# Softmax rows copied by DMA and transposed as fp32r in a hybrid SSD and chunk-band attention step

## The chip, the cores and the metric

The kernel runs on one core of one Trainium2 chip, as a single launch. The metric is the device time of that launch in microseconds (us). The figure before the change is the median of three runs.

## What is computed

One inference step of a two-layer encoder, for 1024 prompt frames and 64 sample frames with a model width of 1024. Layer 0 is a Mamba-2 SSD mixer and a SwiGLU feed-forward part; layer 1 is chunk-band attention and a second SwiGLU part. All arrays are float32. The part that the change touches is the attention of layer 1 (16 heads of 64; chunks of 64 frames; a frame sees its own chunk and the 8 before it):

```python
def band_attend(q, k, v, qpos, kpos, rel_bias):
    dist = jnp.clip(qpos[:, None] - kpos[None, :], -REL_CLIP, REL_CLIP) + REL_CLIP
    bias = rel_bias[:, dist].astype(jnp.float32)
    ...
    s = jnp.einsum('bqhd,bkhd->bhqk', q, k).astype(jnp.float32) * (ATT_HEAD_DIM ** -0.5) + bias
    s = jnp.where(valid, s, -jnp.inf)
    p = jax.nn.softmax(s, axis=-1).astype(v.dtype)
    return jnp.einsum('bhqk,bkhd->bqhd', p, v)
```

## The kernel before

Activations lie with the features on the 128 partitions and the 1088 frames (1024 + 64) along the row. Weights and activations of the large matmuls are split into a rounded fp32r part and its remainder, and each product is made of three fp32r matmuls (L533 to L535 in `passes`).

**The attention stage.** Heads go in pairs, j = 0 to 7, and the frames of a pair in nine blocks of 128 queries, b = 0 to 8 (`att_task(j, b)`, L1975; block 8 is the 64 sample frames, whose keys are mostly the cached ones). A block's keys are 128, 256, 384 and 512 wide for b = 0 to 3 and 640 wide for b = 4 to 8; `w_` is that width and `nkt = w_ / 128`. A block runs in three parts:

- *scores* (L1995 to L2019), for the two heads e = 0 and 1: TensorE writes the scores into a PSUM tile `S` (L2001, L2002, fp32r), VectorE adds the bias and keeps the minimum of the negated scores (L2011), ScalarE takes the exponential and its sum (L2016), VectorE multiplies by the reciprocal (L2017, L2018). The result is the tile `sc` in SBUF, 128 queries by `w_` keys, of which there are four;
- *transposes* (L2028 to L2037): for each head `nkt` transposes of 128 x 128 into a PSUM tile `ptp` (L2032, fp32, with the identity `ident`), which shares its two buffers with `S`; then VectorE (e = 0) or ScalarE (e = 1) copies it to `pT` (L2036);
- *values* (`values`, L2050): the product with V (L2067), made for three blocks at a time, just before the transposes of every third block; the result goes to a DRAM scratch through the tile `ot`.

The keys, values and queries of the next pairs are projected in between (`units`, with `passes`; `evk`, `evq` and `evv` split the results; the lower half of a query remainder is brought to the other partitions by a small DMA, L1942).

**The order of the work.** TensorE's instructions stand in the order in which the program makes them. That order is laid by the class `Stream`: a clock `st.t` advances by the estimated cost of what is issued, and side tasks such as `att_task` are generators that give back a cost, a delay and a condition. `st.pump()`, called between parts of the projection matmuls, lets a side task go on once its delay is over and its condition holds. If the main loop has to wait (`wait_for`), the clock advances by 0.25 at a time without any matmul. After the scores a block's task yields with

```python
yield 1.1 * w_ / 640, AT_W1, lambda: (
    cur["B"] == seqn and st.t >= cur["t"] and (i > 0 or not held or held[0][:2] in v_done)
)
```

so its transposes come at least `AT_W1` = 6.0 of that clock later. `cur["A"]` and `cur["B"]` count the blocks whose scores and transposes are issued; the scores of block n need the transposes of block n - 2 issued, and `GAP_A` and `GAP_B` keep the two kinds of steps apart. The other engines' instructions, and the DMAs that SyncE (SP) issues, are ordered by the framework by priority; `tc.high_priority(ATP)` raises that of the softmax steps. Each queue runs in its order.

**The norms' pool.** `nsb` holds tiles of 128 x 384 fp32 that the RMS norms use: three with the tag `ssum`, two with `sq` and one with `rb`. Between the last norm before the attention and the first one after it they are not used. A tile of a tag is given out in turn; whoever writes it next waits until all readers of its previous use are done.

Of the kernel before, what the change touches and what calls it, by code (L numbers as in the profile page):

```python
# [8 lines left out]
F32 = mybir.dt.float32  # L9
F32R = mybir.dt.float32r  # L10
# [6 lines left out]
P = 128  # L17
# [25 lines left out]
GAP_A, GAP_B = 1.8, 1.2  # L43
RB_WAIT = 4.8
CHW = ((13.1, 8.8, 18.0), (7.5, 6.0, 20.5)), ((9.0, 5.2, 15.0), (10.5, 8.0, 21.0))
AT_W1, AT_W2 = 6.0, 2.5
SSD_GAP, SSD_D = 4.4, 8.0
ST_W, ST_RB = (6.5, 22.0, 22.0), (6.0, 1.0, 1.0)
TB_W, TB_V = 1.0, 10.0
# [375 lines left out]
def hybrid_kernel(  # L425
# [4 lines left out]
    nc = tc.nc  # L430
    V, A, G, PE = nc.vector, nc.scalar, nc.gpsimd, nc.tensor
# [3 lines left out]
    def pool(es, name, bufs=1, **kw):  # L435
        return es.enter_context(tc.tile_pool(reuse_waits="tile", name=name, bufs=bufs, **kw))
# [10 lines left out]
    nsb = pool(ctx, "nsb")  # L447
# [3 lines left out]
    ident = cp.tile([P, P], F32, name="ident")  # L451
# [53 lines left out]
    def rr(ap):  # L505
        return ap.bitcast(F32R)
# [233 lines left out]
    with ExitStack() as es:  # L740
        pyy = es.enter_context(tc.tile_pool(reuse_waits="tile", name="pyy", bufs=4, space=PSUM))
        sb1 = es.enter_context(tc.tile_pool(reuse_waits="tile", name="sb1", bufs=1))
# [335 lines left out]
        for s, (o, n) in enumerate(SL):  # L1078
            xs = []
            if s == 0:  # L1080
                nc.sync.dma_start(pcs, pc)
                for m in range(0, KD, 3):
                    w_ = min(3, KD - m)
# [776 lines left out]
    with ExitStack() as es:  # L1860
        psS = es.enter_context(tc.tile_pool(reuse_waits="tile", name="psS", bufs=2, space=PSUM))
        sb2 = es.enter_context(tc.tile_pool(reuse_waits="tile", name="sba2", bufs=2))
        late = {}
# [27 lines left out]
        def load_bias(j):  # L1891

            bias = []
            for e in range(2):
                bt = late["sb3"].tile([P, WIN], F32, tag="bias", bufs=3, name="bias")
                nc.sync.dma_start(bt, bass.AP(rbrow.tensor, (2 * j + e) * 768, [[1, P], [1, WIN]]))
                G.memset(bt[0:64, 0:64], NEG)
                G.memset(bt[64:128, 576:640], NEG)
                bias.append(bt)
            kqv[j]["bias"] = bias  # L1900
# [74 lines left out]
        def att_task(j, b):  # L1975

            d = kqv[j]
            seqn = j * NCH + b
            s, i = divmod(b, 3)
            yield 0, 0, lambda: (  # L1980
                late and cur["A"] == seqn and cur["B"] >= seqn - 1 and st.t >= cur["t"] and s in d["K"] and s in d["Q"] and (b < 8 or "Ck" in d)
            )
            L = CHL[b]

            if b < 8:
                k0 = max(0, b - 4)
                w_ = P * (b + 1 - k0)
                half = w_ if w_ <= 512 else w_ // 2
                parts = [(c_ // half, d["Kt"], k0 * P + c_, half) for c_ in range(0, w_, half)]
            else:  # L1990
                k0, w_, half = 0, WIN, 512
                parts = [(0, d["Ck"], 0, 512), (1, d["Kt"], 8 * P, P)]
            nkt = w_ // P
            sts = []
            for e in range(2):  # L1995
                sp = psS.tile([P, 2, 512], F32, tag="S", name="S")
                qs = slice(i * P, (i + 1) * P)
                qh, ql = d["Q"][s][e]
                for bank, kd_, ko, fw in parts:
                    dst = sp[:, bank, :fw]  # L2000
                    PE.matmul(dst, qh[:, qs], kd_[e][:, ko:ko + fw], start=True, stop=False)  # L2001
                    at_pe[0] = PE.matmul(dst, ql[:, qs], kd_[e][:, ko:ko + fw], start=False, stop=True)  # L2002
                sc = late["sb3"].tile([P, WIN], F32, tag="sc", bufs=4, name="sc")
                mx = late["sb3"].tile([P, 4], F32, tag="mx", bufs=4, name="mx")
                bt = d["bias"][e]
                brev = bt[:, 0:w_][:, ::-1]

                low = TOP
                with tc.high_priority(ATP):
                    for pi, (f0, f1) in enumerate([(0, half)] + ([(half, w_)] if half < w_ else [])):  # L2010
                        V.tensor_tensor_reduce(  # L2011
                            out=sc[:, f0:f1], in0=sp[:, pi, :f1 - f0], in1=brev[:, f0:f1],
                            scale=-1.0, scalar=low, op0=ALU.add, op1=ALU.min, accum_out=mx[:, pi:pi + 1],
                        )
                        low = mx[:, pi:pi + 1]
                    A.activation(sc[:, :w_], sc[:, :w_], AF.Exp, bias=low, scale=-1.0, accum_out=mx[:, 3:4])  # L2016
                    V.reciprocal(mx[:, 3:4], mx[:, 3:4])  # L2017
                    V.tensor_scalar(sc[:, :w_], sc[:, :w_], mx[:, 3:4], None, op0=ALU.mult)  # L2018
                sts.append(sc)  # L2019
            cur["A"] = seqn + 1  # L2020
            cur["t"] = st.t + 1.1 * w_ / 640 + GAP_A
            yield 1.1 * w_ / 640, AT_W1, lambda: (
                cur["B"] == seqn and st.t >= cur["t"] and (i > 0 or not held or held[0][:2] in v_done)
            )

            cost = values(held) if i == 0 else 0
            PTs = []
            for e in range(2):  # L2028
                pT = late["sb3"].tile([P, 5, P], F32, tag="pT", bufs=6, name="pT")
                pt = psS.tile([P, 2, 512], F32, tag="S", name="ptp").rearrange("p a b -> p (a b)")  # L2030
                for kt in range(nkt):
                    PE.transpose(pt[:, kt * P:(kt + 1) * P], sts[e][:, kt * P:(kt + 1) * P], ident)  # L2032
                ptv = pt[:, :640].rearrange("p (a b) -> p a b", b=P)
                cpf = A.copy if e else V.tensor_copy
                with tc.high_priority(ATP):
                    cpf(pT[:, :nkt, :L], ptv[:, :nkt, :L])  # L2036
                PTs.append(pT)  # L2037
            cur["B"] = seqn + 1
            cost += 1.1 * w_ / 640
            cur["t"] = st.t + cost + GAP_B  # L2040
            held.append((j, s, i, L, nkt, w_, k0, PTs))
            yield cost, 0
            if (j, s) == (7, 2) or (j == 7 and i == 2):

                yield 0, AT_W2, lambda: (j, s) in v_done
                yield values(held), 0
# [3 lines left out]
        def values(blocks):  # L2050

            cost = 0
            while blocks:
                j, s, i, L, nkt, w_, k0, PTs = blocks.pop(0)
                d = kqv[j]
                if i == 0:
                    pos["po"] = ax("po")
                po = pos["po"]
                for kt in range(nkt):
                    for e in range(2):  # L2060
                        if 3 * s + i < 8:
                            vs = d["V"][(k0 + kt) // 3][:, (k0 + kt) % 3, 64 * e:64 * e + 64]
                        elif kt < 4:
                            vs = d["Cv"][:, kt, 64 * e:64 * e + 64]
                        else:
                            vs = d["V"][2][:, 2, 64 * e:64 * e + 64]
                        at_pe[0] = PE.matmul(  # L2067
                            po[64 * e:64 * e + 64, i * P:i * P + L], vs, PTs[e][:, kt, :L],
                            start=(kt == 0), stop=(kt == nkt - 1),
                        )  # L2070
                if i == 2:
                    o, n = SL[s]
                    ot = late["sb1"].tile([P, 384], F32, tag=f"o7{s}" if j == 7 and s < 2 else "ot", name="ot")
                    with tc.high_priority(HIP if j == 7 else 0):
                        A.copy(ot[:, :n], po[:, :n])
                    later(od_[:, j, o:o + n], ot[:, :n], 1.5, lambda: att_done.append((j, s)))
                    if j == 7 and s < 2:
                        last_o[s] = ot
                cur["C"] += 1
                cost += 1.1 * w_ / 640  # L2080
            return cost
# [66 lines left out]
        yY.close()  # L2148
        for nm_, bf in (("sb1", 1), ("sb3", 3)):
            late[nm_] = es.enter_context(tc.tile_pool(reuse_waits="tile", name="sba" + nm_, bufs=bf))  # L2150
        load_bias(0)
        load_side(0)

# [203 lines left out]
```

## Time and profile before

| | |
|---|---|
| median of three runs | 2895.07 us (2892.39 to 2895.51) |
| profiled execution | 2895.43 us, span 2893.7 us |
| mean granted TensorE clock | 0.997 |
| instructions in the span | 57789 |
| attention stage, first to last transpose | 1611 to 2091 us |
| softmax transposes (L2032) | 560, in 72 blocks |

The page of the profile names the engines PE (TensorE matmul), PEld (TensorE weight load, which overlaps PE), DVE (VectorE), ACT (ScalarE), POOL (GpSimd) and SP (SyncE, which here issues DMAs). A group row reads: line, engine, operation, output<-inputs, sizes, count. A matmul's recorded time overlaps that of its neighbours, so the distance between starts tells what one costs in a stream. A timeline row has its start, its length, the engine, and with x10 ten instructions of one kind merged.

### The profile page before, as it was taken

The page shows a single profiled execution, that of the slowest core. Times are in us where ns is not written, and L with a number is a line of the kernel's source. Part 1 is how long each engine was busy: PE and PEld are TensorE (multiplying, and loading weights), DVE is VectorE, ACT ScalarE, POOL GpSimd, SP SyncE. Part 2 cuts the span into 40 slices and gives each one's busy share as a digit, 9 for nine tenths or more (in the row PEclk, how much of TensorE's full clock was granted, in tenths as well). Part 3 has the DMA queues.
Part 4 walks back from the last instruction along what each step waited for, and adds up shares of the span by engine and source line. Part 5 has one row for each costly group of instructions (what it writes and reads, how often), then busy time and mean ns, then how long its engine had stood idle before and what let it go on. Part 6 is the DMA issues. An engine that isn't in the chain of part 4 may idle for free. (4 is left out here: it accounts for less than half of the span.)

```text
span 2893.7 us, 57789 instructions
## 1 busy us (share of the span) xinstructions
PE 2843.4 (98%) x22096; PEld 2799.2 (97%) x22096; DVE 2227.5 (77%) x4739; ACT 1347.6 (47%) x2411; POOL 772.8 (27%) x971
## 2 busy tenths in 40 slices
PE   8999999999999999999999999999999999999999
PEld 8999999999999999999998899999999999999998
DVE  7887888886769877787677677777778877787456
ACT  6654646454454222235444555555564322234442
POOL 1343333330123434351024000000032434343012
PEclk9999999999999999999999999999999999999999
DMA  4433333235556555558875422223377454566555
GB/s 135 129 103 99 105 102 106 94 118 159 174 166 175 163 166 170 174 191 273 286 225 177 131 91 76 65 65 90 97 215 215 136 185 147 183 205 203 193 181 160
DMA packets 284791, 443.23 MB, mean 153 GB/s; under 512 B 25697, under 2 KB 231489, under 8 KB 283105
## 3 DMA queue, kind: packets, MB, share of 16 engines
q1 hardware_dynamic: 275232, 423.47, 45.6%
q0 software_dynamic: 3232, 10.56, 2.1%
q10 hardware_dynamic: 6048, 5.51, 0.6%
q8 instruction: 173, 2.83, 0.4%
q14 instruction: 106, 0.86, 0.1%
HBM read 321.34 MB, written 113.63 MB: 150 GB/s over the span
## 5 line engine op out<-in xcount | busy, mean ns | idle before, releaser
L533 PE MATMUL mm<-r,hl 128*128 128x384 f32 (+2 forms) x1672 | 556.2, 333 | 4.1 <-DMA hl<-kscr 2.4
L535 PE MATMUL mm<-r,hl 128*128 128x384 f32 (+2 forms) x1672 | 539.3, 323 | 1.2 <-DVE hl L389 0.7
L534 PE MATMUL mm<-r,hl 128*128 128x384 f32 (+2 forms) x1672 | 539.2, 322 | 0.0
L1428 PE MATMUL px<-r,hl 128*128 128x288 f32 (+1 forms) x1184 | 347.6, 294 | 0.0
L533 PEld LDWEIGHTS mm<-r,hl 128*128 128x128 f32 x1672 | 316.4, 189 | 6.1 <-DMA hl<-kscr 2.6
L535 PEld LDWEIGHTS mm<-r,hl 128*128 128x128 f32 x1672 | 315.3, 189 | 1.9 <-DVE hl L389 1.0
L534 PEld LDWEIGHTS mm<-r,hl 128*128 128x128 f32 x1672 | 316.2, 189 | 0.3
L1427 PE MATMUL px<-r,hl 128*128 128x288 f32 x1056 | 311.1, 295 | 2.8 <-DVE u L1448 1.6
L1429 PE MATMUL px<-r,hl 128*128 128x288 f32 x1056 | 311.4, 295 | 0.0
L389 DVE TENSOR_TENSOR hl<-raw,hl 128x1024 fp32r<-128x1024 f32 (+2 forms) x186 | 209.6, 1128 | 117.1 <-ACT hl L386 116.8
L559 POOL TENSOR_TENSOR ssum<-ssum,sq 128x256 f32<-128x256 f32 (+1 forms) x111 | 125.0, 1127 | 551.3 <-ACT sq L558 536.3
L386 ACT CAST hl<-raw 128x1024 fp32r<-128x1024 f32 (+2 forms) x186 | 177.5, 955 | 116.2 <-PE po L1770 72.3
L1428 PEld LDWEIGHTS px<-r,hl 128*128 128x128 f32 x1184 | 222.5, 188 | 0.0
L1429 PE MATMUL px<-rx,hl 128*128 128x256 f32 x768 | 214.9, 280 | 2.9 <-DVE hl L389 2.9
L1427 PE MATMUL px<-rx,hl 128*128 128x256 f32 x768 | 214.7, 280 | 0.9 <-DVE u L1442 0.9
L1427 PEld LDWEIGHTS px<-r,hl 128*128 128x128 f32 x1056 | 198.8, 188 | 4.6 <-DVE u L1448 2.0
L1429 PEld LDWEIGHTS px<-r,hl 128*128 128x128 f32 x1056 | 198.8, 188 | 0.1
L1768 PE MATMUL po<-r,hl 128*128 128x288 f32 (+1 forms) x682 | 196.7, 288 | 0.0
L1769 PE MATMUL po<-r,hl 128*128 128x288 f32 (+1 forms) x682 | 196.4, 288 | 0.0
L1770 PE MATMUL po<-r,hl 128*128 128x288 f32 (+1 forms) x682 | 196.4, 288 | 0.0
L1428 PE MATMUL px<-rx,hl 128*128 128x256 f32 x640 | 179.0, 280 | 0.0
L2016 ACT ACTIVATE sc<-sc,mx 128x640 f32<-128x640 f32 (+3 forms) x144 | 101.8, 708 | 106.3 <-DVE mx L2011 103.5
(450 smaller groups left out, 8428.9 us busy)
## 6 DMA issues: line engine op xcount, KB each, us to landing
raw<-in_w_f_dram SPq DMA_DIRECT2D x104, 512.0 KB, 4.0
wsum<-in_w_f_dram SPq DMA_DIRECT2D x128, 176.0 KB, 3.7
wscr<-wsum SPq DMA_DIRECT2D x128, 176.0 KB, 3.3
raw<-in_w_in_dram SPq DMA_DIRECT2D x40, 512.0 KB, 3.7
MT<-ascr SPq DMA_DIRECT2D x48, 384.0 KB, 4.3
raw<-in_w_so_dram SPq DMA_DIRECT2D x32, 512.0 KB, 3.8
r<-hscr SPq DMA_DIRECT2D x22, 576.0 KB, 6.0
hl<-kscr SPq DMA_DIRECT2D x11, 1024.0 KB, 6.1
```

The costliest lines, as they stand in the source:

```text
L386: last = self.nc.scalar.copy(h, v)
L389: (eng or self.eng or self.nc.vector).tensor_tensor(lo, v, h, op=ALU.subtract)
L533: PE.matmul(ps[:, :n], h_, xh, start=(first and i == 0), stop=False)
L534: PE.matmul(ps[:, :n], h_, xl, start=False, stop=False)
L535: at_pe[0] = PE.matmul(ps[:, :n], l_, xh, start=False, stop=(last and i == nk - 1))
L559: (eng or G).tensor_tensor(ssum[:, :n], ssum[:, :n], q[:, :n], op=ALU.add)
L1427: PE.matmul(ps, wh, ah[:, k, :], start=(k == 0), stop=False)
L1428: PE.matmul(ps, wh, al[:, k, :], start=False, stop=False)
L1429: at_pe[0] = PE.matmul(ps, wl, ah[:, k, :], start=False, stop=(k == 3))
L1768: PE.matmul(ps[:, :n], wh, xh, start=(k == 0), stop=False)
L1769: PE.matmul(ps[:, :n], wh, xl, start=False, stop=False)
L1770: at_pe[0] = PE.matmul(ps[:, :n], wl, xh, start=False, stop=(k == KH - 1))
```

## The change

- The constant `AT_WW` = 3.0 / 640 is new. The delay between a block's scores and its transposes is `AT_W1 + AT_WW * w_`, that is 6.6 for a row of 128 and 9.0 for a row of 640.
- After the softmax of each head the row is copied by one DMA (width up to 384) or two (512 and 640) into tiles of `nsb`: the first 384 columns into a tile `ssum`, the rest into a tile `sq`, or `rb` for every third head. SP issues them, under the same raised priority.
- The transposes read these copies instead of `sc`, bitcast to fp32r, with an fp32r copy of the identity (`identr`, made once by ScalarE ahead of the stage), and write the PSUM tile as fp32r. Their number and size stay.

```diff
-AT_W1, AT_W2 = 6.0, 2.5
+AT_W1, AT_W2, AT_WW = 6.0, 2.5, 3.0 / 640
...
                     V.tensor_scalar(sc[:, :w_], sc[:, :w_], mx[:, 3:4], None, op0=ALU.mult)
-                sts.append(sc)
+                    cps = []
+                    for f0, (tag, bufs) in zip(range(0, w_, 384), (("ssum", 3), (("sq", 2), ("rb", 1))[(2 * seqn + e) % 3 == 2])):
+                        cp_ = nsb.tile([P, 384], F32, tag=tag, bufs=bufs, name="pcopy")
+                        nc.sync.dma_start(cp_[:, :min(384, w_ - f0)], sc[:, f0:min(f0 + 384, w_)])
+                        cps.append(cp_)
+                sts.append(cps)
             cur["A"] = seqn + 1
             cur["t"] = st.t + 1.1 * w_ / 640 + GAP_A
-            yield 1.1 * w_ / 640, AT_W1, lambda: (
+            yield 1.1 * w_ / 640, AT_W1 + AT_WW * w_, lambda: (
...
                 for kt in range(nkt):
-                    PE.transpose(pt[:, kt * P:(kt + 1) * P], sts[e][:, kt * P:(kt + 1) * P], ident)
+                    src = sts[e][kt // 3][:, kt % 3 * P:(kt % 3 + 1) * P]
+                    PE.transpose(rr(pt[:, kt * P:(kt + 1) * P]), rr(src), identr)
...
+        identr = late["sb1"].tile([P, P], F32R, name="identr")
+        A.copy(identr, ident)
         load_bias(0)
         load_side(0)
```

## Prediction

> **What bounds the kernel now.** I read the page's first two parts, then the busy times of the attention stage by window, then the groups of that stage by line, then single stretches of the timeline. Page, parts 1 and 2:
>
> ```profile
> PE 2843.4 (98%) x22096; PEld 2799.2 (97%) x22096; DVE 2227.5 (77%) x4739; ACT 1347.6 (47%) x2411; POOL 772.8 (27%) x971
> PEclk9999999999999999999999999999999999999999
> ```
>
> TensorE is the bound over the whole span, and its granted clock never falls. The change touches one stage only: the transposes of the softmax rows (tile ptp) run from 1611 to 2091 us. The window view over that stage, first all instructions, then those of ptp alone (busy us of PE, PEld, DVE, ACT, POOL, then clock, DMA share, GB/s; in the second row PE, PEld, DVE, ACT):
>
> ```profile
> 1600.00:2092.00 492.00, 481.97 (x3905) 464.02 (x3906) 372.16 (x1132) 280.29 (x670) 16.86 (x94) 1.00 0.28 87
> 1600.00:2092.00 492.00, 74.91 (x560) 63.37 (x560) 45.68 (x72) 39.04 (x72) 1.00 0.28 87
> ```
>
> PE sits idle for 492.0 - 482.0 = 10 us in it; VectorE is busy 76%, ScalarE 57%, the DMA engines 28%. So whatever the transposes really cost PE is paid in full, and whatever PE waits for more is paid in full too.
>
> **What a transpose costs PE.** The recorded times of neighbours overlap; the price is the distance between starts. One block of the last head pair, PE's timeline, then PEld's:
>
> ```profile
> 2061.70 0.28 PE L535 MATMUL mm<-r,hl 128*128 128x256 f32 x1
> 2061.82 1.25 PE L2032 MATMUL ptp<-ident,sc 128*128 128x128 f32 x10
> 2062.82 0.37 PE L533 MATMUL mm<-r,hl 128*128 128x256 f32 x1
> 2063.03 0.28 PE L534 MATMUL mm<-r,hl 128*128 128x256 f32 x1
> 2063.15 0.28 PE L535 MATMUL mm<-r,hl 128*128 128x256 f32 x1
> 2061.72 1.11 PEld L2032 LDWEIGHTS ptp<-ident,sc 128*128 128x128 f32 x10
> 2062.80 0.19 PEld L533 LDWEIGHTS mm<-r,hl 128*128 128x128 f32 x1
> ```
>
> Ten transposes start every (2062.80 - 2061.72) / 10 = 0.108 us. From the first to the L534 behind them, less that matmul's usual step of 0.12, the group costs 2063.03 - 2061.82 - 0.12 = 1.09 us.
>
> A step has two halves: the softmax tile is loaded as weights, and the identity streams past it, 128 columns. Which half takes 0.108? A group that begins after a wait shows the load by itself (PEld, one window on the first load, one on the second and third):
>
> ```profile
> 1874.60 0.14 PEld L2032 LDWEIGHTS ptp<-ident,sc 128*128 128x128 f32 x1 [0.17 <-DVE sc L2018]
> 1874.66 0.25 PEld L2032 LDWEIGHTS ptp<-ident,sc 128*128 128x128 f32 x2
> ```
>
> The second load starts 0.06 behind the first; the later ones are held to 0.108 by the stream. So in an fp32 transpose the stream is the slow half. For fp32r the nearest rows are the scores, fp32r with 128 columns (the ninth block of a head pair; PE, then PEld):
>
> ```profile
> 1839.03 0.22 PE L2001 MATMUL S<-K,Qh 128*128 128x128 f32 x1
> 1839.09 0.28 PE L2002 MATMUL S<-K,Ql 128*128 128x128 f32 x1
> 1839.20 0.45 PE L2001 MATMUL S<-Ck,Qh 128*128 128x512 f32 x1
> 1839.03 0.19 PEld L2002 LDWEIGHTS S<-K,Ql 128*128 128x128 f32 x1
> 1839.14 0.19 PEld L2001 LDWEIGHTS S<-Ck,Qh 128*128 128x128 f32 x1
> 1839.25 0.19 PEld L2002 LDWEIGHTS S<-Ck,Ql 128*128 128x128 f32 x1
> ```
>
> An fp32r stream of 128 columns takes 1839.09 - 1839.03 = 0.06 us, but an ordinary fp32r load takes 0.11: the loads come 0.11 apart and hold the third matmul at 0.11.
>
> **The change, part by part.**
>
> *Transposes in fp32r (560 of them, 72 groups).* The trace has no fp32r transpose. Its stream should take 0.06. Its load is bounded by 0.06 (the fp32 transpose's load) and 0.11 (an ordinary fp32r load). I take 0.06, by the recorded durations of one load (ns, the middle one is the median; an fp32 matmul of the first layer that is no transpose, then the transposes):
>
> ```profile
> L987 PEld LDWEIGHTS sp<-xe,Bn x288: 186/192/192, 92.8 to 635.7; 128*128 128x128 f32 x144
> L2032 PEld LDWEIGHTS ptp<-ident,sc x560: 137/140/144, 1611.0 to 2090.8; 128*128 128x128 f32 x187
> ```
>
> An fp32 load that is no transpose takes the same 0.19 us as the fp32r loads above; only a transpose's takes 0.14. So the short load belongs to the transpose and not to fp32. A group of ten then costs 9 x 0.06 + 0.11 (the ordinary load of the matmul behind it has only one short stream to hide under) = 0.65 instead of 1.09. In general each transpose but the last of its group saves 0.049, and the last about 0.01: (560 - 72) x 0.049 + 72 x 0.01 = 24.6 us. With the 0.11 load nothing is saved. A gain above 24.6 is possible where a group begins after a wait: its first step costs some 0.055 more than the others today (1874.60 to 1874.66), up to 72 x 0.055 = 4 us; I take none of it.
>
> The Trainium skill, page TensorE: Matmul & The Clock Gate, section LDWEIGHTS (loading the stationary operand), gives a load as its columns divided by 1.2 per ns, about 107 ns for 128, and makes no exception for a transpose. By that the load bounds both kinds of transpose, and the sum of this part would be about zero. The trace agrees for the scores' loads (0.11) and differs for the transposes' (0.06). The page TensorEngine Tiling (Array Packing), section Restrictions, names a transpose mode for FP32 and FP32R input alike, which fits a short load in both; no run here shows it for fp32r.
>
> *The copies.* Each head of each block gets one DMA, or two where the row is wider than 384: per head pair 2 x (3 + 2 x 6) = 30, in all 240 on SP's queue, 560 x 64 KB = 36.7 MB. Nearest rows (DMA view of the stage: size, median us from issue to landing; then SP's own instruction, ns):
>
> ```profile
> oscr<-ot SPq DMA_DIRECT2D x16, 192.0 KB, 1.9
> Ql<-Ql SPq DMA_DIRECT2D x28, 96.0 KB, 2.1
> L1942 SPq DMA_DIRECT2D Ql<-Ql x48: 461/467/547, 1586.1 to 2051.2; - x48
> ```
>
> A softmax row is there for its transposes some 0.4 + 2.1 = 2.5 us after L2018 (one DMA) or 2.9 (two), instead of at once. What hides it is the distance that PE's order leaves. A wide block, then a ninth block (DVE's rows, then PE's):
>
> ```profile
> 1872.91 0.56 DVE L2018 TENSOR_SCALAR sc<-sc,mx 128x640 f32<-128x640 f32 x1
> 1874.04 0.55 DVE L2018 TENSOR_SCALAR sc<-sc,mx 128x640 f32<-128x640 f32 x1
> 1880.17 1.25 PE L2032 MATMUL ptp<-ident,sc 128*128 128x128 f32 x10
> ...
> 1843.02 0.55 DVE L2018 TENSOR_SCALAR sc<-sc,mx 128x640 f32<-128x640 f32 x1
> 1845.47 0.55 DVE L2018 TENSOR_SCALAR sc<-sc,mx 128x640 f32<-128x640 f32 x1
> 1846.63 1.25 PE L2032 MATMUL ptp<-ident,sc 128*128 128x128 f32 x10
> ```
>
> Wide block: the two heads are ready 6.7 and 6.1 us before their transposes (the second head's begin 0.55 into the group). Ninth block: 3.1 and 1.1 us. So 2.9 us lies inside the distance in the wide block, and in the ninth the second head would be 1.8 late.
>
> *The later transposes (AT_WW).* 3.0 us of the schedule's clock for a row of 640, 0.6 for 128. It adds no instruction; it puts more projection matmuls between a block's scores and its transposes, which are the same matmuls moved forward. In the ninth block 1.1 becomes 4.1, and the copy is covered. What it costs: scores of block n + 2 come after the transposes of block n, so two wide blocks need at least 1.1 (scores) + 6.0 + 3.0 (the wait) + 1.1 (transposes) + 1.2 (GAP_B) = 12.4 of the schedule's clock, whose unit is about a us, against 492 / 72 x 2 = 13.7 us that two blocks take. That is tight but fits; where it doesn't, filler runs short and PE waits a few tenths of a us.
>
> *The ring of copies.* Three sets of tiles: the second head of block n + 1 is copied only when the first head of block n has been transposed. The tightest pair of groups of a head pair (PE):
>
> ```profile
> 1832.64 1.31 PE L2032 MATMUL ptp<-ident,sc 128*128 128x128 f32 x10
> 1835.72 1.15 PE L2032 MATMUL ptp<-ident,sc 128*128 128x128 f32 x9
> ```
>
> Tile free at 1833.2, landed 2.9 later at 1836.1, wanted at 1836.3: no wait, with 0.2 to spare.
>
> *Things at no cost.* The identity's copy (one ACT copy before the stage, hidden while ScalarE is under half busy). DMA traffic: 36.7 MB beside the stage's 42.7 takes the DMA share from 0.28 to some 0.52, hidden as long as weights have their lead. VectorE and ScalarE do the same work in less time: 372 / 468 = 80%; if that cover goes, PE waits for pT copies.
>
> *New waits.* Ends: none, and 8 ninth blocks x 1.8 us plus a quarter of a us in each of the other 64 = 30 us. I take 0.1 us a block, 7 us, nearest to the row of PE's present idle time (10 us over 72 blocks, 0.14 each), since seven blocks of nine have twice the cover that they need.
>
> **Sum**, against the profiled execution (2895.4 us, span 2893.7): 2895.4 - 24.6 + 7 = 2878; the median of the runs is 0.4 lower, so 2877.5.
>
> **Rivals.**
> *The load stays ordinary* (the change doesn't do what it says): fp32r transposes at 0.11. For it: every fp32r load in the trace takes 0.11 or is hidden behind a longer stream. Against it: the 0.06 of the fp32 transposes. Gain 0, waits 0 to 14: 2895 to 2909, likeliest near 2900. The skill's rule on loads leads to the same.
> *SP's queue* (slower). Copies stand in SP's order among DMAs that wait for other engines. SP's waits in the stage:
>
> ```profile
> SPq L494 <- ACT ot L2075: 75.7, 16, 10.4
> SPq L1942 <- DVE Ql L1941: 75.1, 36, 7.6
> SPq L1896 <- DVE mx L2011: 41.0, 13, 4.6
> SPq L283 <- DVE hl L402: 29.1, 11, 4.4
> ```
>
> A copy behind such a wait is late by it, 2.1 us on average behind a Ql. If one block in three were late by that beyond its cover: 24 x 2.1 = 50 us, 2895 - 25 + 50 = 2920. It decides from (24.6 + 6) / 72 = 0.42 us a block. Against it: most of these waits are SP having nothing else to do, and the cover is 6 us in most blocks.
> *VectorE takes over*: PE goes faster and waits for pT copies; half of the gain gone, 2890. Against it: 80% busy, and PE's waits for these copies are small now:
>
> ```profile
> PE S L2001 <- DVE pT L2036: 2.8, 4, 0.9
> ```
>
>
> **How the numbers follow.** What can be told from no change here is 0.2%, 5.8 us. Forecast (2867 to 2887) 0.58; VectorE 0.06, of which two thirds faster; ordinary load 0.21, of which 0.13 within 0.2% and 0.08 slower; SP's queue 0.15, of which 0.13 slower and 0.02 within. Faster 0.62, same 0.17, slower 0.21. The range takes the forecast's low end (24.6 + 4 and no new wait: 2867) and reaches up over the ordinary load's likeliest time, 2901.
>
> **What the changed profile would show.** Right: loads of ptp 0.06 apart, a group of ten in about 0.65, PE waits before ptp under 10 us in all, the stage some 17 us shorter. Ordinary load: 0.11 apart and loads of 0.19. SP's queue: PE's waits before ptp released by DMAs of pcopy, tens of us. The forecast is wrong if the load is ordinary, or if copies land over 4 us after L2018 in many blocks.

## The result, and the profile after

The changed kernel takes 2885.14 us (median; 2881.99 to 2890.66) against 2895.29 for the kernel before, run beside it. The ratio is 0.9965, 95% interval 0.9953 to 0.9977: some 10 us faster. The prediction was 17.6 us, with 2867 to 2901 as its range. The profiled execution took 2884.47 us, 2.0 us of it outside its span. In the new line numbers the copies' DMAs are L2022, the transposes L2038 (were L2032), the copies out of PSUM L2042 (L2036), the value matmuls L2073 (L2067).

Page of the changed kernel, parts 1 and 2:

```profile
PE 2830.8 (98%) x22096; PEld 2784.9 (97%) x22096; DVE 2233.1 (77%) x4739; ACT 1347.0 (47%) x2412; POOL 780.0 (27%) x971
PEclk9999999999999999999999999999999999999999
```

The number of matmuls is the same, and PE's busy time falls by 12.6 us. The same two window rows as before, all instructions and then ptp alone:

```profile
1600.00:2092.00 492.00, 479.89 (x3985) 460.76 (x3984) 378.04 (x1135) 287.09 (x684) 20.39 (x99) 1.00 0.51 164
1600.00:2092.00 492.00, 59.20 (x560) 54.30 (x560) 45.63 (x72) 38.83 (x72) 1.00 0.51 164
```

In the same 492 us PE now gets through 3985 instructions instead of 3905, idles 12.1 us instead of 10.0, and the transposes take 59.2 us of its records instead of 74.9. The DMA share goes from 0.28 to 0.51, as foreseen (0.52). From the first score matmul to the last value matmul the stage shrinks from 492.7 to 484.0 us; the rest of the difference lies in stages that the change does not touch. Part of the 10 us may be clock and not the change: in the profiled execution of before the clock record falls to 0.50 for 3.4 us each at 1579, 1606 and 2245 us, in that of the changed kernel at none of these places. Half the clock for 3.4 us loses 1.7 us, so that is 3 x 1.7 = 5 us of the 11 between these two executions. Over all runs the mean clock is 0.9978 for the changed kernel and 0.9972 for the kernel before (the 60 runs beside the experiments), which is some 2 us.

One block, PE's timeline and PEld's (start, duration, then engine, line and tile), to set beside the group at 2061 us of before:

```profile
1819.50 0.97 PE L2038 MATMUL ptp<-identr,pcopy 128*128 128x128 f32 x10
1820.31 0.41 PE L533 MATMUL mm<-r,hl 128*128 128x384 f32 x1
1820.56 0.34 PE L534 MATMUL mm<-r,hl 128*128 128x384 f32 x1
1819.33 1.00 PEld L2038 LDWEIGHTS ptp<-identr,pcopy 128*128 128x128 f32 x10
1820.27 0.19 PEld L533 LDWEIGHTS mm<-r,hl 128*128 128x128 f32 x1
1820.38 0.19 PEld L534 LDWEIGHTS mm<-r,hl 128*128 128x128 f32 x1
```

From the first transpose to the L534 behind, less that matmul's usual 0.175: 1820.56 - 1819.50 - 0.175 = 0.885 us. Before it was 1.09, forecast was 0.65. The distance between starts of two transposes is 0.085 (median of 488); it was 0.109, and 0.06 was forecast. The first two steps of a group behind projections take 0.06, so the nine steps of this one take 0.72 in all. Groups that come behind value matmuls cost 0.95: their first step takes 0.115 and their second 0.087.

The tile view of ptp (ns: min/median/max) and one row of its "sat idle before it until" (us, times):

```profile
L2038 PEld LDWEIGHTS ptp<-identr,pcopy x560: 137/141/144, 1609.9 to 2083.3; 128*128 128x128 f32 x187
L2038 PE MATMUL ptp<-identr,pcopy x560: 221/250/306, 1610.0 to 2083.3; 128*128 128x128 f32 x187
  DMA pcopy<-sc: 0.3, 1
```

The load keeps the transpose's short record (141 ns, not the ordinary 190), and in the whole stage PE waited once, 0.3 us, for a copy. PE's present waits are others: PEld's waits in the stage,

```profile
PEld S L2001 <- DVE pT L2042: 6.7, 11, 1.2
PEld S L2001 <- ACT pT L2042: 2.6, 10, 0.4
```

are scores that wait for the copies of ptp out of PSUM, because S and ptp share two buffers. In the new order nine groups of ten are followed directly by scores (three groups before), and such a group costs 1.59 at the median, 0.7 of it this wait.

DMA view of the stage (size, median us from issue to landing), then SP's waits (us, times, longest):

```profile
pcopy<-sc SPq DMA_DIRECT2D x112, 192.0 KB, 2.2
pcopy<-sc SPq DMA_DIRECT2D x96, 128.0 KB, 2.1
pcopy<-sc SPq DMA_DIRECT2D x32, 64.0 KB, 2.1
SPq L2022 <- DVE sc L2018: 162.4, 83, 4.6
SPq L2022 <- PE ptp L2038: 22.3, 37, 1.6
SPq L1942 <- DVE Ql L1941: 8.0, 14, 1.9
```

SP waits 162 us for softmax rows and is otherwise little held; the ring of copies holds it 22 us, 37 times, and nothing on PE follows from it.

### The profile page after: what moved, and what is told of

Same layout as the page of the kernel before. It is cut to its first block, busy times and chain, and to the rows that moved or that the text cites. A ratio compares the mean times of both kernels' runs of the same rounds, so it can differ in the third digit from the quotient of the medians.

```text
span 2882.4 us, 58508 instructions
## 1 busy us (share of the span) xinstructions
PE 2830.8 (98%) x22096; PEld 2784.9 (97%) x22096; DVE 2233.1 (77%) x4739; ACT 1347.0 (47%) x2412; POOL 780.0 (27%) x971
## 5 line engine op out<-in xcount | busy, mean ns | idle before, releaser
L534 PE MATMUL mm<-r,hl 128*128 128x384 f32 (+2 forms) x1672 | 538.7, 322 | 0.0
L534 PEld LDWEIGHTS mm<-r,hl 128*128 128x128 f32 x1672 | 315.4, 189 | 0.0
```

Of the source, the lines that this page charges most:

```text
L534: PE.matmul(ps[:, :n], h_, xl, start=False, stop=False)
```

## The experiments

What stands at stake: what an fp32r transpose takes and which half of it sets that; what the copies and the later order cost; and whether either is worth having alone. Times are medians in us, ratios are to the kernel before, run beside each. "PE idle" is 492 less the PE busy time of the window 1600 to 2092 us, and the clock is that window's.

| kernel | time | ratio (95%) | PE idle | clock |
|---|---|---|---|---|
| before | 2895.29 | | 10.0 | 1.00 |
| changed | 2885.14 | 0.9965 (0.9953 to 0.9977) | 12.1 | 1.00 |
| fp32 from the copies | 2898.70 | 1.0016 (1.0008 to 1.0025) | 13.7 | 1.00 |
| not later | 2907.17 | 1.0037 (1.0025 to 1.0050) | 25.4 | 0.99 |
| later only | 2909.89 | 1.0051 (1.0037 to 1.0065) | 23.6 | 1.00 |
| fp32 in own tiles, later | 2896.62 | 1.0004 (0.9995 to 1.0012) | 10.9 | 1.00 |
| plain matmul | 2918.50 | 1.0086 (1.0069 to 1.0103) | 20.3 | 0.97 |
| spread | 2940.56 | 1.0164 (1.0149 to 1.0179) | 37.2 | 0.96 |
| half later | 2927.66 | 1.0110 (1.0096 to 1.0123) | 35.0 | 0.97 |
| no DMA, no delay | 2881.05 | 0.9954 (0.9942 to 0.9967) | 9.3 | 1.00 |
| no DMA, a third later | 2899.16 | 1.0018 (1.0008 to 1.0029) | 20.7 | 0.98 |
| no DMA, full delay | 2887.20 | 0.9974 (0.9965 to 0.9983) | 12.5 | 0.99 |

**fp32 from the copies.** The changed kernel, with its transposes put back to fp32.

```diff
-                    PE.transpose(rr(pt[:, kt * P:(kt + 1) * P]), rr(src), identr)
+                    PE.transpose(pt[:, kt * P:(kt + 1) * P], src, ident)
```

> The copies and the later transposes stay, the transposes go back to fp32 with the fp32 identity. Theory A (the gain is the shorter fp32r step, 0.085 us a transpose instead of 0.109, and copies and order cost next to nothing): the steps are 0.109 again and the time is that of before plus the few us of new waits, 2895 to 2899. Theory B (the gain comes from the new order, the later transposes with more matmuls in between; fp32r is beside the point): as after, about 2885.

2898.70, ratio 1.0016 (1.0008 to 1.0025); the steps are 0.109 again. PEld's waits in the stage:

```profile
PEld S L2001 <- ACT pT L2042: 8.3, 12, 1.3
PEld S L2001 <- DVE pT L2042: 5.1, 10, 1.0
```

So copies and later order together cost some 4 us (PE idles 3.7 us more), and these rows carry it: the scores' wait for ptp's buffers is 13.4 us here and 5.9 us (3.9 for VectorE's copies, 2.0 for ScalarE's) in the kernel before. The type alone is worth 2898.7 - 2885.1 = 13.5 us, near 488 x (0.109 - 0.085) = 11.7.

**Half the stream, fp32 and fp32r.** Which half of a step is slow? In both kernels the blocks of 64 rows are cut to their 64 partitions: the load keeps its 128 columns (on 64 partitions), the stream has 64 instead of 128.

```diff
-                    PE.transpose(pt[:, kt * P:(kt + 1) * P], sts[e][:, kt * P:(kt + 1) * P], ident)
+                    PE.transpose(pt[:, kt * P:kt * P + L], sts[e][:L, kt * P:(kt + 1) * P], ident[:L, :L])
```

The other is the same cut in the changed kernel.

> The kernel before; in the ninth block, whose queries are 64, the fp32 transposes take 64 partitions and stream 64 identity columns instead of 128 (the other 64 rows are not used further on). If the stream bounds an fp32 transpose (0.108) and its load takes 0.06, the step in these blocks falls to about 0.06 and their groups of ten to 0.6 to 0.75. If the load bounds it, as the rule of 107 ns for 128 columns has it, the step stays 0.109.

> The changed kernel with the same cut in the ninth block: fp32r transposes of 64 partitions that stream 64 columns. If the load bounds an fp32r transpose (it takes 0.085), the step in these blocks stays 0.085. If the step is the stream plus a fixed part (0.056 + 0.029), it falls to about 0.057.

Single executions took 2891.65 and 2893.60 us; it is the steps that count here. A group of such a block on PEld, first fp32, then fp32r:

```profile
1720.40 0.70 PEld L2032 LDWEIGHTS ptp<-ident,sc 64*128 64x128 f32 x10 [0.25 <-DVE K L1918]
```

```profile
1728.45 0.89 PEld L2038 LDWEIGHTS ptp<-identr,pcopy 64*128 64x128 f32 x10 [0.25 <-DVE sc L2018]
```

The last load lasts 0.14, so ten loads start (0.70 - 0.14) / 9 = 0.062 apart in fp32 and (0.89 - 0.14) / 9 = 0.083 in fp32r. Halving the stream takes the fp32 step from 0.109 to 0.062 and leaves the fp32r step where it was: fp32 transposes are held by the stream, fp32r ones by something that the length of the stream does not change. The load is the half that kept its columns; a fixed part of each step that belongs to neither half is not excluded.

**Plain matmul.** Is the short load the transpose's? The same product with the identity, as an ordinary fp32r matmul.

```diff
-                    PE.transpose(rr(pt[:, kt * P:(kt + 1) * P]), rr(src), identr)
+                    PE.matmul(pt[:, kt * P:(kt + 1) * P], rr(src), identr, start=True, stop=True)
```

> The changed kernel with an ordinary fp32r matmul by the identity in place of each transpose (fp32r products, so the probabilities are rounded). If the short load belongs to the transpose mode, loads are recorded at 0.19, come 0.11 apart, a group of ten costs 1.1 and the gain is gone: 2894 to 2898. If the 0.085 belongs to fp32r with 128 columns as such, the step and the time stay as after, 2885.

2918.50, ratio 1.0086 (1.0069 to 1.0103). The tile view, PEld's timeline of one group, and the stage's window:

```profile
L2038 PEld LDWEIGHTS ptp<-identr,pcopy x560: 186/192/192, 1613.5 to 2119.1; 128*128 128x128 f32 x187
1703.52 1.26 PEld L2038 LDWEIGHTS ptp<-identr,pcopy 128*128 128x128 f32 x10
1704.70 0.19 PEld L533 LDWEIGHTS mm<-r,hl 128*128 128x128 f32 x1
1600.00:2092.00 492.00, 471.66 (x3653) 455.67 (x3651) 362.76 (x1090) 272.20 (x649) 15.03 (x93) 0.97 0.47 155
```

Loads of the ordinary kind (192 ns) come 0.112 apart, in the same type and from the same tiles: the short load is the transpose's. The time is 20 us above what the step explains. Against the changed kernel the span is 35.9 us longer: 488 x 0.027 = 13 for the steps, 8.2 more idle time, and some 14 of clock (a mean of 0.972 over 492 us). The clock was in nobody's expectation; it comes back below.

**Not later.** The changed kernel with the old delay.

```diff
-AT_W1, AT_W2, AT_WW = 6.0, 2.5, 3.0 / 640
+AT_W1, AT_W2, AT_WW = 6.0, 2.5, 0.0
```

> AT_WW = 0, all else as after. By the prediction's cover sums: in the ninth block of each head pair the second head's copy comes 1.8 us late, 8 x 1.8 = 14 us, less where PE's order gives more room; time 2890 to 2898, with PE's waits ahead of the transposes released by DMAs of pcopy. Rival: the copies are covered by the room that the order has anyway and AT_WW buys nothing: 2885, waits on pcopy under 2 us.

2907.17, ratio 1.0037 (1.0025 to 1.0050), 22 us above the changed kernel and 9 above the expected range. Rows of ptp's "sat idle before it until":

```profile
  DMA pcopy<-sc: 15.1, 19
  DVE sc L2018: 9.1, 12
  issue: 7.9, 19
```

Waits for an uncovered copy are there, 15.1 us in 19 waits. That the total is near the 14 us worked out for the eight ninth blocks is in part luck: by PE's order some 10 us of it stand in the ninth blocks, 3.8 of these in a single wait, and 5 in others. PE idles 13.3 us more than in the changed kernel, and 0.01 x 492 = 5 us of clock go too; the span of the profiled execution, the fastest of five, is 17.0 us longer.

**Later only.** The kernel before with the new delay, no copies.

```diff
-            yield 1.1 * w_ / 640, AT_W1, lambda: (
+            yield 1.1 * w_ / 640, AT_W1 + 3.0 / 640 * w_, lambda: (
```

> The kernel before with the longer delay alone (6.0 + 3.0 x width / 640), no copies, fp32 transposes. Theory A: no change, 2893 to 2898. Theory B (order): most of the gain, about 2885 to 2888.

2909.89, ratio 1.0051 (1.0037 to 1.0065): a miss, 15 us slower where about nothing was expected, and PE idles 13.6 us more. A wait of PEld and one of VectorE, with the same VectorE row of before behind them:

```profile
PEld ptp L2032 <- DVE mx L2011: 15.5, 15, 2.2
DVE Ck L1882 <- ACT Ck L1881: 27.8, 9, 3.8
```

```profile
DVE Ck L1882 <- ACT Ck L1881: 7.4, 9, 1.4
```

My reading was that a row that waits longer for its transposes holds its sc tile longer. There are four, and the cached keys (cr) are loaded into the same four; their preparation then comes late (27.8 us of waits instead of 7.4) and with it the rows. The next kernel tests that.

**fp32 in own tiles, later.** No DMA: VectorE's last softmax step writes the copies' tiles instead of sc, in fp32; transposes fp32, full delay.

```diff
-                    V.tensor_scalar(sc[:, :w_], sc[:, :w_], mx[:, 3:4], None, op0=ALU.mult)
...
-                        nc.sync.dma_start(cp_[:, :min(384, w_ - f0)], sc[:, f0:min(f0 + 384, w_)])
+                        V.tensor_scalar(cp_[:, :min(384, w_ - f0)], sc[:, f0:min(f0 + 384, w_)], mx[:, 3:4], None, op0=ALU.mult)
...
-                    PE.transpose(rr(pt[:, kt * P:(kt + 1) * P]), rr(src), identr)
+                    PE.transpose(pt[:, kt * P:(kt + 1) * P], src, ident)
```

> The later delay and fp32 transposes, no DMA, but VectorE's last softmax step writes the rows into the tiles of the norms' pool, in fp32. If the 15 us of the later order alone came from the four sc tiles (held until the later transposes, so that the next rows and the cached keys, which share the tag, come late), they go: 2893 to 2899, as with the copies. If they came from the later order itself, 2908 to 2912. The difference to the copies with fp32 transposes (2898.7) is then the price of the DMAs: 0 to 5 us.

2896.62, ratio 1.0004 (0.9995 to 1.0012), and both rows are back where they were (1.7 us for the second in the kernel before):

```profile
DVE Ck L1882 <- ACT Ck L1881: 8.0, 9, 2.0
PEld ptp L2037 <- DVE mx L2011: 0.6, 1, 0.6
```

With the rows in tiles of their own the late order costs 13 us less than with rows in sc. The copies thus do a second service: they free sc early. Against the fp32 kernel with DMAs (2898.70) the DMAs themselves would cost some 2 us; the intervals overlap, so this is not shown.

**Spread.** If the load is the slow half, one transpose behind each projection matmul might hide it. The transposes go into a list; `passes` takes one after each matmul, and the main loop one each time that it has to wait.

```diff
+    tq = []
+
+    def pop():
+        if tq:
+            tq.pop(0)()
+            st.t += 0.055
...
+                for kt in range(nkt):
+                    tq.append(lambda e=e, kt=kt: step(e, kt))
```

> The changed kernel with the transposes spread: one behind each projection matmul instead of ten in a row (same copies, same number, a block's transposes are kept in a list from which the projections take one after each matmul). If a transpose is bound by its load, which only a short stream hides, it can hide under the 0.16 us stream of a projection matmul: a pair costs 0.22 to 0.235 instead of 0.175 + 0.085 = 0.26, 560 x 0.025 to 0.04 = 14 to 22 us less, 2863 to 2871. If changing between the two modes of load costs what the end of a group shows (the matmul after the first one behind a group starts 0.07 late), a pair costs 0.3 or more: 2900 to 2925.

2940.56, ratio 1.0164 (1.0149 to 1.0179): the slowest of all, 15 us above the higher of the two ranges. PE's timeline among projections, then where the projections run out, then the stage's window:

```profile
1623.98 0.22 PE L2053 MATMUL ptp<-identr,pcopy 128*128 128x128 f32 x1
1624.04 0.36 PE L545 MATMUL mm<-r,hl 128*128 128x320 f32 x1
1624.24 0.22 PE L2053 MATMUL ptp<-identr,pcopy 128*128 128x128 f32 x1
1790.76 0.84 PE L2053 MATMUL ptp<-identr,pcopy 128*128 128x128 f32 x5 [2.80 <-DMA pcopy<-sc]
1600.00:2092.00 492.00, 454.76 (x3503) 433.05 (x3503) 348.08 (x1049) 258.51 (x623) 14.94 (x93) 0.96 0.45 147
```

A projection of 320 columns with a transpose takes 1624.24 - 1623.98 = 0.26 instead of its 0.15: 0.11 for one transpose (306 such), more than 0.085 in a group. My reading is that the ordinary load behind the transpose has only its short stream to hide under, so that every transpose pays the exit that a group pays once. The rest are waits, 25 us more idle time than in the changed kernel, where the transposes were taken too early for their copies, and 0.04 x 492 = 20 us of clock.

**Half later.** The changed kernel with AT_WW = 1.5 / 640.

```diff
-AT_W1, AT_W2, AT_WW = 6.0, 2.5, 3.0 / 640
+AT_W1, AT_W2, AT_WW = 6.0, 2.5, 1.5 / 640
```

> The changed kernel with AT_WW = 1.5 / 640. With 0 the transposes wait for copies (2907), with 3.0 PE goes from transposes straight to scores nine times and waits for the copies out of PSUM there (2885). If both costs fall off on the way, 2881 to 2885; if the copies' waits come back in proportion, 2890 to 2897.

2927.66, ratio 1.0110 (1.0096 to 1.0123): a miss. The time is not monotone in the delay (0: 2907, 1.5: 2928, 3.0: 2885). Windows of its trace, the stage and two neighbours of 3.4 us, and PE's timeline in the first of these two:

```profile
1600.00:2092.00 492.00, 456.96 (x3589) 435.99 (x3587) 350.04 (x1072) 263.70 (x635) 15.29 (x93) 0.97 0.47 151
1927.80:1931.20 3.40, 1.99 (x17) 1.59 (x16) 2.61 (x8) 2.48 (x6) 0.29 (x2) 1.00 0.92 287
1931.20:1934.60 3.40, 3.36 (x20) 2.73 (x21) 2.55 (x11) 2.09 (x9) 0.00 (x0) 0.50 0.60 193
1927.80 0.97 PE L2038 MATMUL ptp<-identr,pcopy 128*128 128x128 f32 x10
1929.34 0.33 PE L2001 MATMUL S<-K,Qh 128*128 128x128 f32 x1 [0.57 <-DVE pT L2042]
1931.05 0.38 PE L2038 MATMUL ptp<-identr,pcopy 128*128 128x128 f32 x2 [0.82 <-DVE mx L2011]
```

Against the changed kernel the span is 43.3 us longer: 22.9 us more idle time and 0.03 x 492 = 15 us of clock give 38 of it. The idle time was in the expectations of neither theory in that size, and the clock in none. The clock rows show how the two hang together: the two waits leave PE 1.99 of 3.40 us busy (59%), and in the next 3.4 us the granted clock is 0.50. The changed kernel's emptiest window behind the first 15 us of the stage, and the one behind that:

```profile
2022.80:2026.20 3.40, 2.35 (x20) 2.16 (x18) 3.13 (x9) 1.05 (x4) 0.00 (x0) 1.00 0.99 310
2026.20:2029.60 3.40, 3.38 (x62) 3.06 (x62) 2.72 (x10) 3.28 (x9) 0.00 (x0) 1.00 0.41 109
```

69% busy, and the clock stays. (Two windows in its first 15 us, at 1602.9 and 1609.8 us, are emptier, 52% and 53%, and the clock stays there too.) Why this order has more short waits than those at 0 and 3.0 is not settled: the planner turns the delay into another sequence (eleven groups of ten go straight to scores instead of nine), and its waits lie in many places.

**No DMA, no delay.** As in the kernel with fp32 rows in own tiles, but VectorE writes them as fp32r, the transposes stay fp32r, and AT_WW = 0.

```diff
-                        nc.sync.dma_start(cp_[:, :min(384, w_ - f0)], sc[:, f0:min(f0 + 384, w_)])
+                        V.tensor_scalar(rr(cp_[:, :min(384, w_ - f0)]), sc[:, f0:min(f0 + 384, w_)], mx[:, 3:4], None, op0=ALU.mult)
```

> No DMA copies: VectorE's last softmax step writes the tiles of the norms' pool itself, as fp32r, in one or two instructions, so the probabilities are rounded to fp32r (the copies keep them as they are); AT_WW = 0. Theory A: steps of 0.085 as after, no wait for a copy, 96 more VectorE instructions: 2882 to 2886. If the DMAs or the later order had a price that the after trace hides (SP's queue, DMA traffic), the time falls further, to 2880 or less. Theory B: 2895.

2881.05, ratio 0.9954 (0.9942 to 0.9967), the lowest of all; its interval overlaps the changed kernel's, so the 4 us between them are not shown. No copies to wait for, the order of before, and PE idles less than in the kernel before:

```profile
1600.00:2092.00 492.00, 482.75 (x4018) 466.20 (x4017) 385.81 (x1234) 287.11 (x688) 21.23 (x101) 1.00 0.30 92
```

**No DMA, a third later, and full delay.** The same with AT_WW = 1.0 / 640 and 3.0 / 640.

> VectorE writes the rows as fp32r into the pool's tiles (rounded, no DMA), with AT_WW = 1.0 / 640 instead of 0. The remaining waits of that kernel ahead of scores and transposes are some 10 us. If a little more room helps, 2876 to 2880; if the room is there already, 2880 to 2884.

> The changed kernel with its full delay (3.0 for a row of 640), but VectorE's last softmax step writes the pool tiles itself, rounded to fp32r, in place of the write in sc and the DMA; the low bits of the probabilities are left out. It differs from the kernel with fp32 rows in pool tiles (2896.6) by the type of the transposes alone, and from the changed kernel (2885.1) by the DMAs alone. Theory A (prices add: fp32r transposes are worth 13.5 us wherever they stand, the DMAs cost about 2): 2881 to 2885, steps of 0.085, PE waits before S for pT copies near those of the changed kernel (9 us on PEld). Theory B (the time jumps with the order that the planner happens to produce, as it did at a delay of 1.0, 2899, and of 1.5 with DMAs, 2928): above 2890, with several groups of transposes followed directly by scores or by one another, and a granted clock below 1.00 in the attention stage.

A third later: 2899.16, ratio 1.0018 (1.0008 to 1.0029), a miss, 15 us above the higher of the two ranges. Two groups of ten now stand next to each other seven times, followed by scores:

```profile
PEld ptp L2037 <- ACT pT L2041: 8.7, 7, 1.4
```

```profile
1600.00:2092.00 492.00, 471.34 (x3858) 454.27 (x3856) 383.62 (x1227) 280.43 (x670) 15.87 (x94) 0.98 0.29 87
```

11 us more idle time than without a delay and some 7 of clock (means of 0.983 and 0.997), against 18 in the medians. Full delay: 2887.20, ratio 0.9974 (0.9965 to 0.9983), 2 us above the expected range, and not to be told from the changed kernel: there the DMAs cost nothing that these runs show. Against the fp32 kernel in the same tiles and order (2896.62) the type is worth 9.4 us.

## Why the prediction came out as it did

- **PE as the bound of the stage: right.** Every kernel here follows the same sum: what transposes cost, what PE idles, and what its clock loses. The last part was missing in the forecast: "its granted clock never falls" was read from slices of 72 us, in which half the clock for 3.4 us does not show. The clock record of before has five such windows.
- **The short load as a property of the transpose: right, but the type counts too** (0.083 us between loads in fp32r, 0.062 at most in fp32). The fp32r transpose's load is recorded at 141 ns, the plain matmul's at 192. The rival of the ordinary load is what the plain matmul shows: 0.112 a step, and no gain. The rule of the Trainium skill (TensorE: Matmul & The Clock Gate, LDWEIGHTS), columns / 1.2 per ns, gives an estimate of 107 ns for 128 columns; the trace agrees for the ordinary loads (0.112) and for no transpose.
- **The step of 0.06: the term that was mis-sized.** I took the load of an fp32r transpose from the fp32 one, because the two records have the same length. The distance between starts is 0.085, in the middle of the bounds 0.06 and 0.11. With it the term is 488 x 0.024 = 11.7 us instead of 24.6. Measured with all else equal it is 13.5 us (with DMAs) and 9.4 (without). The two come together when idle time and lost clock are taken off the stage, as shown below: 11.3 and 12.6.
- **The exit of a group: somewhat more than forecast.** In the group shown the nine steps take 0.72, so 0.885 leaves 0.17 for the last transpose and the ordinary load behind it, against 0.11. (With nine steps of 0.085 it would be 0.12; the first two are shorter.)
- **The copies' cover: right.** One wait of 0.3 us; 15.1 us without the later order, where 14 had been worked out. Of the 15.1 some 10 stand in the ninth blocks, for which the 14 were meant.
- **New waits, 7 us: about right** (4 us, by the kernel with fp32 from the copies; 2 to 7 by its interval), but for another reason than copies that come late: groups that run straight into scores and wait for ptp's PSUM buffers. The rival in which VectorE takes over names the same wait; here the order makes it.
- **The later order at no cost: right only together with the copies.** The prediction did not price that copies free sc earlier. Alone, the later order costs 15 us.
- **SP's queue: right that it costs nothing on PE.** The rival of 2920 has no row: one wait of 0.3 us for a copy.

13.5 - 4 gives the measured gain again, but by construction: both figures are differences to the same third kernel. The profiled stages are a check of their own. The stage from the first score matmul to the last value matmul, less PE's idle time and less what half-clock windows took of it, is 481 to 485 us in the four kernels with fp32 transposes of full size (before, fp32 from the copies, later only, fp32 in own tiles) and 468 to 474 in the six with fp32r transposes in groups (changed, not later, half later, and the three without DMA). So in every order fp32r is worth about 12 us of PE's work, near 488 x 0.024, where 24.6 had been forecast. From before to changed this part falls by 9.1 us (481.0 to 471.9); 2.1 more idle time and the half-clock window at 1606 us, 1.7 us that the changed kernel does not lose, make it the 8.7 us by which the stage shrinks. The direction came from the mechanism that was forecast; the gain is 10 instead of 17.6 us because a step saves half of what was put down for it.

## What to carry to other kernels

The price of a pipelined instruction is the distance between starts, and equal records (140 and 141 ns here) do not mean equal distances; a short test that halves one half, stream or load, says which one holds it. A delay in an order has to be priced with the buffers that it keeps full, and a copy made for one reason may pay by freeing them. A planner's parameter is tried at several values: here the middle one was worse than both ends.

## What the hardware showed that was not expected

**The fp32r transpose's load.** 0.083 to 0.085 us apart, between the fp32 transpose's (0.062 or less) and the ordinary load (0.112). What makes the difference is open.

**Half-clock windows in a busy stage.** The clock record falls to 0.50 for 3.4 or 6.8 us at a time, on a fixed grid of 3.4 us. Worked out from the records of all fourteen traces between 1600 and 2110 us, for windows of this grid at full clock: none of those in which PE was busy 69% or more was followed by one at half clock, all of those with 46% or less were, and between these both occur. Inside the stage the changed kernel has none. The half-later kernel loses 15 us in six places, and the plain matmuls lose theirs in six too: one at the start of the stage and five that lie 65 to 68 us apart, one per head pair, where a group runs straight into scores. No gap needs to be long: in the window shown above the longest waits are 0.57 and 0.82 us. The Trainium skill (TensorE: Matmul & The Clock Gate, HAM oscillation) tells of gaps over some 3.4 us; the rows here differ from that, and agree with its window's length and the half clock. Read so, waits of PE are paid twice from a certain density on; no run here changed the density alone, and what decides between 47 and 68% is open. It also bears on the scatter: the changed kernel's executions of 2881.99 and 2890.66 us have a mean clock of 0.999 and 0.996, and 0.003 x 2885 is 8.7 us, the difference between them.
